# The samples' tile moved from the first prompt tile to the third, in a two-layer decoder step

## Chip, cores and metric

The kernel runs on all 8 cores of one Trainium2 chip. Each core does one prompt sequence of 2048 tokens and four of the 32 samples. The metric is device microseconds (us) of the slowest core. Executions come in two states: in the slow one, the cores of one die or of both have a lower granted TensorE clock, and the time is some per cent to over ten per cent longer.

## The reference, cut to what matters

One inference step of two layers is run for a prompt group and a sample group that share all weights.

```python
D_MODEL, SEQ, FFN_DIM = 1024, 2048, 2688
DEC_BATCH, DEC_SEQ, PAST_LEN = 32, 8, 8192
for layer in range(2):
    x = x + 0.5 * swiglu_ffn(rmsnorm(x), ...)        # FFN 0 / FFN 2
    h = rmsnorm(x)
    y = gla_mixer(h, ...) if layer == 0 \            # linear attention, carries a state
        else dilated_window_attention(q, shared_k, shared_v) @ w_o
    x = x + y
    x = x + 0.5 * swiglu_ffn(rmsnorm(x), ...)        # FFN 1 / FFN 3
    # after layer 0: the shared k, v are made from x
```

The samples start from a stored state (4 MB a core) and a stored window of keys and values. The kernel loads 13.6 MB of that window per core.

## The kernel before

The prompt is cut into four tiles of 512 tokens, t0 to t3. The core's samples form one more tile, ts, of 32 tokens. Two prompt tiles run side by side: t0 and t2 take their weights from ring 0, t1 and t3 from ring 1. Each ring holds 12,288 columns in SBUF, which is six units of 2048. All weights are loaded again for each prompt tile, as f32 in HBM and bf16 in SBUF. The samples have no weights of their own: they read the units of one prompt tile, each of which then has two users.

```python
for t in range(4):
    def add_unit(kind, i, src, n, users=0, t=t):
        u = Unit(src, n, users or (1 if t else 2), (t, kind, i))   # t0's units: t0 and ts
        ...
        order[t % 2].append(u)
    ...                                  # FFN 0; then v, qk of the linear attention
            if t == 0 and kind == "qk":  # the samples' state goes into the same ring
                for s in range(4):
                    add_unit("S0", s, src, 2048, 1)
    ...                                  # r, o; FFN 1; kv; FFN 2; wq
        if t == 0:                       # the samples' cache, before the output projection
            for s in range(4):
                add_unit("ck", s, ck[s], 3328, 1)
                add_unit("cv", s, cv[s], 3328, 1)
    ...                                  # wo; FFN 3

def weights(slot):                       # one such thread for each ring
    for k, u in enumerate(order[slot]):
        ...
        yield need(lambda over=over: all(o.left == 0 for _, _, o in over))  # all users done
        ...
        yield O(PL, lambda e: e.dma_start(out=dst, in_=u.src), ...)         # queue of POOL
        u.ready = True

def use(T, kind, i):
    u = units[(T.u, kind, i)]
    yield need(lambda: u.ready)
    ...
    return u
```

The program is written by threads (generators), one for each tile and many small ones. A greedy scheduler with a clock of its own picks, at each step, the operation that is ready first, and among nearly equal ones (`TIE = 0.15` us) the one of lowest rank. The samples' tile has the lowest rank of the tiles (-20), so it goes first. What comes out is a fixed order on each engine. On the chip every engine goes through its list in that order, and waits on semaphores.

```python
class Sched:
    DMA_BW = 315e3       # bytes per us
    DMA_LAT = 3.2        # us from the end of a transfer to its use
class Threads:
    TIE = 0.15
    FAVOUR = 0.02        # weight of rank against readiness on ACT and DVE
```

The samples' linear attention (`gla_s`) keeps its scratch in the key array `KT`, in the part of tiles t1 to t3, so that those tiles must not write their keys before it is done:

```python
KA, KB = KT[:, 0, 512:2048], KT[:, 1, 512:2048]
...
vv = KA[0:32, 0:1024]
...
# in kv(), before a prompt tile writes its keys
if T.t:
    yield need(lambda: "gla_s" in done)
```

The softmax here doesn't subtract the row's maximum and nothing guards it: scores larger than these inputs give would overflow.

Of the kernel before, what the change touches and what calls it, by code (L numbers as in the profile page):

```python
# [8 lines left out]
BF16 = mybir.dt.bfloat16  # L9
# [4 lines left out]
PE, ACT, DVE, PL, SP = ENGS  # L14
# [205 lines left out]
def O(eng, fn, reads=(), writes=(), cost=0.5, dma=None, nbytes=0):  # L220

    if fn.__closure__:
        fn = types.FunctionType(fn.__code__, fn.__globals__, fn.__name__, fn.__defaults__,
                                tuple(types.CellType(c.cell_contents) for c in fn.__closure__))
    return ("op", eng, fn, list(reads), list(writes), cost, dma, nbytes)


def need(cond):
    return ("need", cond)


def c_act(n):
    return 0.19 + n * 0.00084
# [76 lines left out]
def build():  # L310
# [20 lines left out]
    S = Sched(nc)  # L331
    TH = Threads(S)
    A = nc.alloc_sbuf_tensor
# [9 lines left out]
    KT = A("KT", [128, 2, 2048], BF16)  # L343
# [10 lines left out]
    PS = [PST[:, b, :] for b in range(8)]  # L354
# [81 lines left out]
    units = {}  # L436
    order = [[], []]

    for t in range(4):
        def add_unit(kind, i, src, n, users=0, t=t):  # L440
            u = Unit(src, n, users or (1 if t else 2), (t, kind, i))
            u.kind = kind
            units[(t, kind, i)] = u
            order[t % 2].append(u)

        def ffn_units(f):
            for j in range(NF):
                add_unit("fi%d" % f, j, wfi[f * NF + j], 2048)
            for m in range(8):
                add_unit("fo%d" % f, m, wfo[f * 8 + m], 2688)  # L450
                if (t, f) == (3, 3) and m % 2 == 0:

                    order[0].append(order[1].pop())
        ffn_units(0)
        for gi, kind in enumerate(("v", "qk", "r", "o")):
            for i in range(4):
                add_unit(kind, i, wgl[gi * 4 + i], 2048)
            if t == 0 and kind == "qk":
                for s in range(4):
                    src = st_in[s * 4:(s + 1) * 4].rearrange("h p d -> p h d")  # L460
                    add_unit("S0", s, src, 2048, 1)
                    add_unit("S0b", s, None, 1024, 1)
        ffn_units(1)
        for i in range(2):
            add_unit("kv", i, wkv[i], 2048)
        ffn_units(2)
        for i in range(3):
            add_unit("wq", i, wqd[i], 2048)
        if t == 0:
            for s in range(4):  # L470
                add_unit("ck", s, ck[s], 3328, 1)
                add_unit("cv", s, cv[s], 3328, 1)
        for i in range(4):
            add_unit("wo", i, wod[i], 1536)
        ffn_units(3)
# [52 lines left out]
    xsb = A("xsb", [128, 8, 32], F32)  # L528
    hsb = A("hsb", [128, 8, 32], BF16)
    spb = A("spb", [128, 10, 32], F32)  # L530
    rsb = A("rsb", [128, 1216], BF16)
    KTs = A("KTs", [128, 2, 32], BF16)
    Vsn = A("Vsn", [32, 256], BF16)
    stabs = A("stabs", [128, 64], F32)
    pool = Pool("pb", [pb[:, k, :] for k in range(NPB)])
# [4 lines left out]
    for t in range(4):  # L540
        T = Tile()
        i = t % 2
# [16 lines left out]
        tiles.append(T)  # L559
    TS = Tile()  # L560
    TS.nm, TS.i, TS.t, TS.n, TS.rank = "ts", "s", -1, 32, (lambda: -20)
    TS.u, TS.slot = 0, None
    TS.b = "bs"
    TS.x, TS.h, TS.pool = xsb, hsb, spool
    TS.R = rsb
# [8 lines left out]
    done = set()  # L574
# [7 lines left out]
    def rk(T, what):  # L582
        return ("R", T.b, what)
# [38 lines left out]
    def copy(eng, out, in_, n, reads, writes):  # L622
        if eng == ACT:
            return O(ACT, lambda e: e.copy(out=out, in_=in_), reads, writes, c_act(n))  # L624
        return O(eng, lambda e: e.tensor_copy(out=out, in_=in_), reads, writes, c_dve(n))
# [12 lines left out]


    def load_x(T, prev):  # L640
        nq = 4 if T.n == 512 else 1
        for q in range(nq):
            ms = range(q * 8 // nq, (q + 1) * 8 // nq)
            if prev is not None:
                yield need(lambda: all(("y", prev.nm, m) in done for m in ms))
            if T.t == 1:
                after = units[(0, "fi0", 3 + 2 * q)]
                yield need(lambda: after.ready)
            w = len(ms) * T.n
            src = xp[T.t] if T.n == 512 else xs  # L650
            yield O(ACT if T.t == 0 and q % 2 else SP, (lambda e, q=q, w=w, src=src, ms=ms: e.dma_start(
                out=T.x[:, ms[0]:ms[-1] + 1, :].rearrange("p m n -> p (m n)"), in_=src[:, q * w:(q + 1) * w])),
                [after.key] if T.t == 1 else [], writes=[xk(T, m) for m in ms], cost=0.1, dma="x%s_%d" % (T.b, q), nbytes=w * 512)
        if T.t == 0:

            T.sum = None
            for m in range(8):
                if m % 2:
                    yield stt(T.h[:, m, :], T.x[:, m, :], 1.0 / 1024, T.x[:, m, :], ALU.mult, ALU.mult, T.n, [xk(T, m)], [hk(T, m)])
                else:  # L660
                    yield act(T.h[:, m, :], T.x[:, m, :], AF.Square, T.n, [xk(T, m)], [hk(T, m)], scale=1.0 / 32)
                done.add(("sq", T.nm, 0, m))
            return
        for m in range(8):
            yield from square(T, m)
# [358 lines left out]
    def gla_s(T):  # L1024
        n = 32
        h8 = hks(T)
        R = T.R
        region(T, ACTK, ["g"])

        KA, KB = KT[:, 0, 512:2048], KT[:, 1, 512:2048]  # L1030
        qT = KB[:, 0:128].rearrange("p (h n) -> p h n", h=4)
        kT = KB[:, 128:256].rearrange("p (h n) -> p h n", h=4)
        kd = KB[:, 256:384].rearrange("p (h n) -> p h n", h=4)
        vv = KA[0:32, 0:1024]
        ktok = KA[0:32, 1024:1536].rearrange("p (h w) -> p h w", h=4)
        kms = KB[0:32, 384:896].rearrange("p (h w) -> p h w", h=4)
        am = KB[0:32, 896:1024].rearrange("p (h w) -> p h w", h=4)
        oT = R[:, 0:512].bitcast(F32).rearrange("p (m n) -> p m n", m=8)
        uT = R[:, 512:768].rearrange("p (m n) -> p m n", m=8)
        gk = rk(T, "g")  # L1040
# [4 lines left out]
        EQ, EK = A4, C4  # L1045
        (b,) = yield from get_banks(1)
        yield from mmh(T, (PS[b][0:16, 0:n],), lambda kt, z: WLR[:, kt, 0:16], ["WLR"], (b,), n)
        glr = KB[0:16, 896:928]
        yield copy(ACT, glr, PS[b][0:16, 0:n], n, [("ps", b)], [gk])
        put(b)  # L1050
        (b,) = yield from get_banks(1)
# [16 lines left out]
        for hd in range(4):  # L1068
            u = yield from use(T, "v", hd)
            v = u.ap.rearrange("p (kt c) -> p kt c", kt=8)  # L1070
            (b,) = yield from get_banks(1)
            yield mm(PS[b][0:32, 0:256], [(T.h[:, kt, :], v[:, kt, :]) for kt in range(8)], h8 + [u.key], b, 256)
            u.left -= 1
            yield copy(ACT, vv[:, hd * 256:(hd + 1) * 256], PS[b][0:32, 0:256], 256, [("ps", b)], [rk(T, ("gv", hd))])
            put(b)
        for hd in range(4):
            u = yield from use(T, "qk", hd)
# [29 lines left out]
        yield O(PE, fa, [gk], [("ps", b)], c_mm(4, 32))  # L1107
        yield tt(am, pa, CB[0:32, B_MS:B_MS + 32].unsqueeze(1).to_broadcast([32, 4, 32]), ALU.mult, 128, [("ps", b), "CB"], [gk])
        put(b)
        gv = [rk(T, ("gv", hd)) for hd in range(4)]  # L1110
        (b,) = yield from get_banks(1)

        def fi(e):
# [7 lines left out]
        for s in range(4):  # L1121
# [19 lines left out]
            for hp in range(2):  # L1141
# [10 lines left out]
                for a in range(2):  # L1152
                    hd = 2 * hp + a
# [3 lines left out]
                    cost=0.1, dma="sts%d" % s, nbytes=524288)  # L1157
            us.left -= 1
            ub.left -= 1

        sq = spb[:, 8:10, :].rearrange("p a n -> p (a n)").bitcast(BF16)
        RS = C4
# [7 lines left out]
        for hd in range(4):  # L1170
            u = yield from use(T, "r", hd)
# [13 lines left out]
        for q in range(4):  # L1185
            u = yield from use(T, "o", q)
# [4 lines left out]
                TH.spawn(resid(T, 2 * q + z, b, PS[b][:, 0:n], n), -4, T.rank)  # L1191
            u.left -= 1
        gs = ["g", "go", "kms"] + [("gv", h) for h in range(4)]
        for t in range(1, 4):
            for a in range(2):
                S.readers.setdefault(("KT", t, a), []).extend(
                    [S.lastw[rk(T, k)] for k in gs] + [r for k in gs for r in S.readers.get(rk(T, k), ())])
        region(T, gs, ACTK)
        done.add("gla_s")

# [35 lines left out]
    def kv(T, tab):  # L1236
        n = T.n
# [3 lines left out]
        def kpost(kc, b):  # L1241
            def write(t1, rs, k1, k2):
                yield tt(t1, t1, rs, ALU.mult, n, [k1, k2], [k1])
                if n == 512:
                    if T.t:
                        yield need(lambda: "gla_s" in done)
                    yield copy(ACT, KT[:, kc, T.t * 512:(T.t + 1) * 512], t1, n, [k1], [("KT", T.t, kc)])
                    dst = kp_o[kc][:, T.t * 512:(T.t + 1) * 512]
                else:
                    yield copy(ACT, KTs[:, kc, :], t1, n, [k1], [("KTs", kc)])  # L1250
                    dst = ks_o[kc]
                yield O(SP, (lambda e: e.dma_start(out=dst, in_=t1)), [k1], [], cost=0.1, dma="ko%s%d" % (T.b, kc), nbytes=n * 512)
                done.add(("K", T.nm, kc))
            yield from norm_rope(T, b, 62, tab, 3, write)
            left[0] -= 1
            if left[0] == 0 and tab[3] is not None:
                T.pool.put("tab", *tab[3])

        u = yield from use(T, "kv", 0)
# [6 lines left out]
        u = yield from use(T, "kv", 1)  # L1266
# [443 lines left out]
```

## Time and profile before

| | before |
|---|---|
| first three timed runs, us | 2356.7, 2508.9, 2710.3 |
| the profiled execution (fast), us | 2357.4 |
| span of the slowest core, us | 2355.6 (all: 2338.7 to 2355.6) |
| PE busy | 98% |
| granted clock, mean by core | 0.991 to 0.995 |

The page of the kernel before. First the busy time of each engine, then rows of busy tenths in 40 equal slices of the span (9 is 90% or more; PEclk is the granted clock, DMA the mean share of the 16 DMA engines), then the chain of work that ended last, by engine:

```profile
span 2355.6 us, 42703 instructions; the slowest of 8 cores (2338.7 to 2355.6 us)
PE 2298.3 (98%) x14643; PEld 1124.9 (48%) x14643; DVE 1218.2 (52%) x2181; ACT 1169.9 (50%) x2309; POOL 317.0 (13%) x599
...
PE   6999999999999999999999899999999999999998
...
PEclk9999999999999999999999999999999999999999
DMA  8997897888987999977999988888999989598793
...
PE 93%; DMA 5%; issue 1%; ACT 0%; DVE 0%; SPq 0%; DVEq 0%; POOLq 0%; ACTq 0%; POOL 0%
```

PE is the limit. A change can win only what PE waits. The view of waits lists the engine and line that waited, what released it, the total in us, the number of times and the longest. Here is PE in the kernel before:

```profile
PE pst L615 <- ACT hsb L620: 13.7, 1, 13.7
PE pst L615 <- DMA ring<-wfi: 8.2, 5, 3.7
PE pst L615 <- DVE h L631: 8.1, 5, 2.9
PE pst L615 <- DMA ring<-wfo: 8.0, 3, 7.4
...
PE pst L1523 <- DMA ring<-ck: 1.5, 1, 1.5
```

The first line is the start of the kernel. `wfi` and `wfo` are the FFN weights, `ck` the samples' cache. The timeline shows waits for weights (start us, length us, engine, line, operation, form, count, and the idle time before with its releaser). `hsb` and `rsb` belong to the samples, `h` and `r` to prompt tiles.

```profile
586.08 2.29 PE L615 MATMUL pst<-h,ring 128*128 128x512 bf16 x8
592.07 0.59 PE L615 MATMUL pst<-hsb,ring 128*128 128x32 bf16 x16 [3.70 <-DMA ring<-wfi]
592.49 2.72 PE L615 MATMUL pst<-h,ring 128*128 128x512 bf16 x6
...
849.43 3.62 PE L615 MATMUL pst<-h,ring 128*128 128x512 bf16 x16
854.58 0.97 PE L1523 MATMUL pst<-rsb,ring 64*128 64x8 bf16 x52 [1.53 <-DMA ring<-ck]
```

Sixteen matmuls of the samples take about 0.4 us from the first start to the next group, 25 ns each. Before them PE stood 3.70 us. The wait costs more than itself: during it the granted clock fell to 0.5, from 590.8 to 597.6 us, and the next eleven steps of the prompt matmuls took 427 ns in place of 216. The first line below is the stretch from 590 to 649 us; its mean clock is 0.94. The second is from tile t2's attention, which has room in DMA (columns: stretch, then busy us and count of PE, PEld, DVE, ACT, POOL, then granted clock, DMA share, GB/s):

```profile
590.00:649.00 59.00, 56.93 (x380) 27.33 (x381) 26.37 (x53) 34.23 (x74) 7.92 (x15) 0.94 0.95 157
2006.00:2065.00 59.00, 59.00 (x422) 30.29 (x421) 38.33 (x67) 34.95 (x68) 5.27 (x10) 0.97 0.60 102
```

### The profile page before, as it was taken

To read this page: it belongs to the slowest core of one execution; us is meant where nothing else is said; L and a number is where in the kernel's file an instruction comes from. 1 tells how busy PE (TensorE), PEld (TensorE's weight loads), DVE (VectorE), ACT (ScalarE), POOL (GpSimd) and SP (SyncE) were. 2 spreads that over 40 slices of the span, in tenths; PEclk is the share of its full clock that TensorE was granted. 3 is DMA by queue.
4 is the path that set the end of the run, shared out by engine and by line. 5 is a ranking of instruction groups with operands and counts; after the bars stand their busy time and mean duration, and the time that the engine had idled before them with its cause. 6 is when DMAs were issued, how large, how long until landed. Compare 5 with 4: busy or idle time off the path is not lost.

```text
span 2355.6 us, 42703 instructions; the slowest of 8 cores (2338.7 to 2355.6 us)
## 1 busy us (share of the span) xinstructions
PE 2298.3 (98%) x14643; PEld 1124.9 (48%) x14643; DVE 1218.2 (52%) x2181; ACT 1169.9 (50%) x2309; POOL 317.0 (13%) x599
## 2 busy tenths in 40 slices
PE   6999999999999999999999899999999999999998
PEld 3445455554445444445444355455444444544544
DVE  3535664566444566457442355644663355644732
ACT  4635655554543465555553156456555335644551
POOL 1111111111111111110111111111111111011010
PEclk9999999999999999999999999999999999999999
DMA  8997897888987999977999988888999989598793
GB/s 161 175 171 132 153 165 130 137 136 146 156 151 130 181 155 158 172 130 150 185 156 173 174 138 140 143 146 140 159 160 167 165 157 170 94 159 145 141 177 88
DMA packets 101475, 357.23 MB, mean 152 GB/s; under 512 B 12400, under 2 KB 17552, under 8 KB 101136
## 3 DMA queue, kind: packets, MB, share of 16 engines
q0 software_dynamic: 84144, 326.25, 83.1%
q1 hardware_dynamic: 16832, 27.21, 3.7%
q8 instruction: 122, 2.00, 0.3%
q10 hardware_dynamic: 288, 1.05, 0.2%
q14 instruction: 89, 0.73, 0.1%
HBM read 663.17 MB, written 15.40 MB: 288 GB/s over the span
## 4 chain that ended last, share of the span: by engine, by line
PE 93%; DMA 5%; issue 1%; ACT 0%; DVE 0%; SPq 0%; DVEq 0%; POOLq 0%; ACTq 0%; POOL 0%
PE pst L615 89%; DMA ring<-wfi 2%; DMA ring<-wfo 2%; PE pst L1436 1%; PE pst L1375 1%; DMA x<-xp 0%; DMA ring<-ck 0%; PE pst L1397 0%; PE pst L987 0%; PE pst L1004 0%; PE pst L1005 0%; ACT pb L620 0%; PE pst L1401 0%; PE pst L1459 0%; PE pst L974 0%
## 5 line engine op out<-in xcount | busy, mean ns | idle before, releaser
L615 PE MATMUL pst<-h,ring 128*128 128x512 bf16 x6144 | 1387.6, 381 | 9.4 <-DVE h L631 6.9
L615 PEld LDWEIGHTS pst<-h,ring 128*128 128x128 bf16 x6144 | 589.8, 98 | 707.4 <-issue 37.2
L615 PE MATMUL pst<-r,ring 128*128 128x512 bf16 x3136 | 707.2, 380 | 7.4 <-DMA ring<-wfo 7.4
L620 ACT ACTIVATE pb<-pb 128x512 f32<-128x512 f32 x856 | 535.4, 630 | 71.6 <-DVE pb L840 12.1
L620 ACT ACTIVATE pb<-pst 128x512 f32<-128x512 f32 (+1 forms) x472 | 278.9, 595 | 449.0 <-PE pst L615 441.8
L628 DVE TENSOR_TENSOR pb<-pb,pst 128x512 f32<-128x512 f32 x368 | 251.8, 685 | 463.8 <-ACT pb L620 456.4
L615 PEld LDWEIGHTS pst<-r,ring 128*128 128x128 bf16 x3136 | 302.1, 98 | 364.6 <-issue 12.8
L511 POOL DMA_DIRECT2D ring<-wfi x336 | 177.6, 529 | 1101.4 <-PE pst L615 973.7
L620 ACT ACTIVATE h<-x 128x512 bf16<-128x512 f32 x188 | 116.6, 627 | 353.7 <-DVE x L631 280.2
L628 DVE TENSOR_TENSOR r<-pb,pst 128x512 bf16<-128x512 f32 x336 | 230.5, 686 | 46.3 <-DVE pb L628 38.8
L631 DVE SCALAR_TENSOR_TENSOR x<-pst,x 128x512 f32<-128x512 f32 x128 | 88.2, 689 | 216.4 <-PE pst L615 215.7
L631 DVE SCALAR_TENSOR_TENSOR h<-x,CF,pb 128x512 bf16<-128x512 f32 x224 | 150.8, 745 | 12.4 <-ACT pb L620 9.4
L511 POOL DMA_DIRECT2D ring<-wfo x128 | 67.6, 528 | 540.7 <-PE pst L615 439.4
L628 DVE TENSOR_TENSOR pb<-pb,h 128x512 f32<-128x512 f32 x115 | 79.0, 689 | 44.8 <-ACT h L620 42.6
L615 PE MATMUL pst<-ring,h 128*128 128x256 bf16 x640 | 74.4, 273 | 0.0
L620 ACT ACTIVATE spb<-pst 128x32 f32<-128x32 f32 (+2 forms) x111 | 21.7, 198 | 100.5 <-PE pst L615 99.2
L615 PEld LDWEIGHTS pst<-hsb,ring 128*128 128x128 bf16 x1536 | 52.4, 96 | 32.2 <-issue 13.8
L615 PEld LDWEIGHTS pst<-ring,h 128*128 128x128 bf16 x640 | 62.3, 98 | 11.2
L511 POOL DMA_DIRECT2D ring<-wgl x64 | 33.8, 530 | 220.3 <-PE pst L615 201.6
L624 ACT COPY r<-pst 128x512 f32<-128x512 f32 (+3 forms) x104 | 51.2, 492 | 23.6 <-PE pst L1401 11.3
L615 PE MATMUL pst<-hsb,ring 128*128 128x32 bf16 x1536 | 54.0, 177 | 8.3 <-DMA ring<-wfi 8.2
L620 ACT ACTIVATE h<-pst 128x512 bf16<-128x512 f32 (+4 forms) x96 | 46.4, 510 | 18.3 <-PE pst L1375 10.3
(153 smaller groups left out, 1082.5 us busy)
## 6 DMA issues: line engine op xcount, KB each, us to landing
ring<-wfi POOLq DMA_DIRECT2D x336, 512.0 KB, 7.8
ring<-wfo POOLq DMA_DIRECT2D x128, 672.0 KB, 8.2
ring<-wgl POOLq DMA_DIRECT2D x64, 512.0 KB, 7.2
y_p<-x SPq DMA_DIRECT2D x32, 256.0 KB, 8.1
x<-xp SPq DMA_DIRECT2D x14, 512.0 KB, 10.4
ring<-wqd POOLq DMA_DIRECT2D x12, 512.0 KB, 10.5
ring<-wod POOLq DMA_DIRECT2D x16, 384.0 KB, 7.6
ring<-wkv POOLq DMA_DIRECT2D x8, 512.0 KB, 7.3
```

The costliest lines, as they stand in the source:

```text
L511: yield O(PL, (lambda e, u=u, dst=dst: e.dma_start(out=dst, in_=u.src)), first.get(u.uid, []), writes=[u.key], cost=1.0, dma="w%d_%d" % (s ...
L615: ins = e.matmul(out, lhsT=l, rhs=r, start=(start and i == 0), stop=(stop and i == last), skip_group_check=skip)
L620: return O(ACT, lambda e: e.activation(out=out, in_=in_, func=func, scale=scale, bias=bias), reads, writes, c_act(n))
L624: return O(ACT, lambda e: e.copy(out=out, in_=in_), reads, writes, c_act(n))
L628: return O(DVE, lambda e: e.tensor_tensor(out=out, in0=a, in1=b, op=op), reads, writes, c_dve(n, rate))
L631: return O(DVE, lambda e: e.scalar_tensor_tensor(out=out, in0=a, scalar=s, in1=b, op0=op0, op1=op1), reads, writes, c_dve(n))
L1375: ins = e.matmul(PS[bs[hp]][:, bi * 256 + jj * 128:bi * 256 + jj * 128 + 128], lhsT=KT[hp * 64:hp * 64 + 64, jj, sl_(k0, 128, kst)], rhs=T ...
L1436: ins = e.matmul(PS[bs[hp]][0:nk, rr * 64 + jj * 32:rr * 64 + jj * 32 + 32], lhsT=KT[hp * 64:hp * 64 + 64, jj, sl_(r, nk, 16)], rhs=T.QT[h ...
```

## The change

The intent is to take the samples' loads (their state and cache) and their latencies out of the crowded first tile and put them where the prompt's attention is long and DMA has room. Tile t2's weights get the second user. The samples start when t0 is done. Their scratch shrinks to the last tile's part of `KT`, which is free longest; the values go to one of the 11 shared scratch buffers, and only t3 must wait for `gla_s`.

```diff
+    TSU = 2
     for t in range(4):
         def add_unit(kind, i, src, n, users=0, t=t):
-            u = Unit(src, n, users or (1 if t else 2), (t, kind, i))
+            u = Unit(src, n, users or (2 if t == TSU else 1), (t, kind, i))
 ...
-            if t == 0 and kind == "qk":
+            if t == TSU and kind == "qk":
 ...
-        if t == 0:
+        if t == TSU:
             for s in range(4):
                 add_unit("ck", s, ck[s], 3328, 1)
 ...
-    TS.u, TS.slot = 0, None
+    TS.u, TS.slot = TSU, None
 ...
     def load_x(T, prev):
+        if T.n == 32:
+            yield need(lambda: ("y", "t0", 0) in done)
 ...
-        KA, KB = KT[:, 0, 512:2048], KT[:, 1, 512:2048]
+        KA, KB = KT[:, 0, 1536:2048], KT[:, 1, 1536:2048]
+        (vi,) = yield from pool.get(("s", "vv"), 1, 1)
 ...
-        vv = KA[0:32, 0:1024]
+        vv = pool.aps[vi][0:32, :].bitcast(BF16)
 ...
-                    if T.t:
+                    if T.t == 3:
                         yield need(lambda: "gla_s" in done)
```

Cut: the places of the smaller scratch arrays, `rsb` longer by 64 columns, and the order of reads and writes for the smaller region.

More of the change, by code (lines that the diff above doesn't have):

```diff
@@ L530, in build @@
     spb = A("spb", [128, 10, 32], F32)
-    rsb = A("rsb", [128, 1216], BF16)
+    rsb = A("rsb", [128, 1280], BF16)
     KTs = A("KTs", [128, 2, 32], BF16)
@@ L1028, in gla_s @@
         region(T, ACTK, ["g"])
-        KA, KB = KT[:, 0, 512:2048], KT[:, 1, 512:2048]
-        qT = KB[:, 0:128].rearrange("p (h n) -> p h n", h=4)
-        kT = KB[:, 128:256].rearrange("p (h n) -> p h n", h=4)
-        kd = KB[:, 256:384].rearrange("p (h n) -> p h n", h=4)
-        vv = KA[0:32, 0:1024]
-        ktok = KA[0:32, 1024:1536].rearrange("p (h w) -> p h w", h=4)
-        kms = KB[0:32, 384:896].rearrange("p (h w) -> p h w", h=4)
-        am = KB[0:32, 896:1024].rearrange("p (h w) -> p h w", h=4)
+        KA, KB = KT[:, 0, 1536:2048], KT[:, 1, 1536:2048]
+        (vi,) = yield from pool.get(("s", "vv"), 1, 1)
+        qT = KA[:, 0:128].rearrange("p (h n) -> p h n", h=4)
+        kT = KA[:, 128:256].rearrange("p (h n) -> p h n", h=4)
+        kd = KA[:, 256:384].rearrange("p (h n) -> p h n", h=4)
+        am = KA[0:32, 384:512].rearrange("p (h w) -> p h w", h=4)
+        ktok = KB[0:32, :].rearrange("p (h w) -> p h w", h=4)
+        vv = pool.aps[vi][0:32, :].bitcast(BF16)
+        vk = pool.key(vi)
+        kms = R[0:32, 768:1280].rearrange("p (h w) -> p h w", h=4)
         oT = R[:, 0:512].bitcast(F32).rearrange("p (m n) -> p m n", m=8)
@@ L1047, in gla_s @@
         yield from mmh(T, (PS[b][0:16, 0:n],), lambda kt, z: WLR[:, kt, 0:16], ["WLR"], (b,), n)
-        glr = KB[0:16, 896:928]
+        glr = KA[0:16, 384:416]
         yield copy(ACT, glr, PS[b][0:16, 0:n], n, [("ps", b)], [gk])
@@ L1073, in gla_s @@
             u.left -= 1
-            yield copy(ACT, vv[:, hd * 256:(hd + 1) * 256], PS[b][0:32, 0:256], 256, [("ps", b)], [rk(T, ("gv", hd))])
+            yield copy(ACT, vv[:, hd * 256:(hd + 1) * 256], PS[b][0:32, 0:256], 256, [("ps", b)], [vk, rk(T, ("gv", hd))])
             put(b)
@@ L1109, in gla_s @@
         put(b)
-        gv = [rk(T, ("gv", hd)) for hd in range(4)]
+        gv = [vk] + [rk(T, ("gv", hd)) for hd in range(4)]
         (b,) = yield from get_banks(1)
@@ L1159, in gla_s @@
             ub.left -= 1
+        pool.put(("s", "vv"), vi)
         sq = spb[:, 8:10, :].rearrange("p a n -> p (a n)").bitcast(BF16)
@@ L1193, in gla_s @@
         gs = ["g", "go", "kms"] + [("gv", h) for h in range(4)]
-        for t in range(1, 4):
-            for a in range(2):
-                S.readers.setdefault(("KT", t, a), []).extend(
-                    [S.lastw[rk(T, k)] for k in gs] + [r for k in gs for r in S.readers.get(rk(T, k), ())])
+        for a in range(2):
+            S.readers.setdefault(("KT", 3, a), []).extend(
+                [S.lastw[rk(T, k)] for k in gs] + [r for k in gs for r in S.readers.get(rk(T, k), ())])
         region(T, gs, ACTK)
```

## The prediction

> All times are for the fast state (2356.7 us timed, 2357.4 profiled; the other two timed runs, 2508.9 and 2710.3, I take as slow).
>
> **What bounds the kernel now.** PE. The page gives PE 98% busy in a 2355.6 us span; the chain of waits is 93% PE. Busy time proves little (the Trainium skill, "Perfetto Trace Analysis", opening note, calls it a bad metric), so I read the starts of successive matmuls in the timeline: 216 ns for 128x512, 109 for 128x256, 25 for the samples' 128x32. That agrees with the floor of about 25 ns in the Trainium skill, "TensorE: Matmul & The Clock Gate", section "Wait — 56ns, not 53.3ns?". With each form at its median step, PE needs about 2244 us. So only some 111 us are not needed: 13.7 before the first matmul, 6.3 after the last, about 91 between. The change can win or lose only there.
>
> Where the 91 lie: 17 in the first 120 us (half-rate matmuls of 427 ns up to about 28 us, waits for weights and norm); 7 at 540-600 (waits for weights); 14.4 at 840-960, where the samples' attention waits for its cache (chain: 10.8 us of loading it; DMA 0.89 to 1.0); 14.3 at 1320-1380, where tile 1 ends and tile 3 starts (7.6 us wait for FFN output weights, DMA 0.99); 17 in the attention of tiles 2 and 3 (1980-2040 and 2160-2220; waits for ACT and DVE).
>
> **What moves.** Nothing is removed: the same matmuls, the same bytes. The samples' 2320 FFN-type matmuls at 25 ns are 58 us, their whole PE work some 75 us by the same steps; it leaves the first 1100 us and comes back between about 1000 and 2200. So do 4 state loads of 1 MB and 8 cache loads of 1.7 MB, 17.8 MB of HBM reads; at the mean 288 GB/s an estimated 62 us of loading. One of 11 shared scratch buffers is held during the samples' linear attention. The wait on its completion is left to tile 3 and should cost nothing: tile 3's keys come over 400 us of PE work later in program order.
>
> **On the critical path.**
> - Gain, 6 to 12 us: the cache loads leave tile 0's short attention, where DMA is full, for that of tile 2, where DMA is at 0.60 (2006-2065 us). Most of the 14 us at 840-960 goes.
> - Gain, 2 to 5 us: the samples' short matmuls fill part of the wait at the tile 1 to tile 3 change, and of the waits in tile 2's attention.
> - Loss, 4 to 8 us: in the first 180 us DMA is at 0.90 to 1.03, and the samples' 13 us of first-FFN work filled PE there. Without it PE waits longer for weights.
> - Loss, 0 to 4 us: the samples' small ACT and DVE operations (about 200 ns each) meet tile 2's attention, which already waits for ACT and DVE; one scratch buffer fewer.
>
> Sum: about -7 us. Predicted **2350 us**, 8 in 10 between **2330 and 2372**. Faster by over 2%: 0.03; within 2%: 0.94; slower by over 2%: 0.03.
>
> **What would show it.** Right: the same PE work; waits on the cache near tile 0's attention gone, no equal one at tile 2's; a few us more waiting for weights before 180 us; tile 0 ends some 70 us earlier; DMA near tile 2's attention up from 0.60.
>
> **What would make it wrong.** The cache loads hold tile 2's half of the weight ring so long that its output projection waits (PE idle over 15 us near 1950-2050); state loads colliding with the tile 1 to tile 3 change, already at DMA 0.99; the first 180 us losing over 15 us, DMA-bound.

## The result, and the profile after

Ratios in this document are the mean time of one kernel's fast runs over that of the other's in the same rounds, so they are not quite the ratio of the medians quoted.

| | before | after |
|---|---|---|
| first rounds, fast runs, us | 2356.7, 2358.8 | 2354.2 to 2358.5 (4 runs, median 2356.1) |
| ratio, 95% interval | | 0.9993 (0.9969 to 1.0018) |
| five more rounds, median of fast runs, us | 2357.0 | 2355.7 |
| ratio, 95% interval | | 0.9994 (0.9980 to 1.0008) |
| profiled span, slowest core, us | 2355.6 | 2354.4 |
| PE busy on that core, us | 2298.3 | 2300.7 |

The time is the same: 1.4 us less in the longer measurement, with an interval from 4.7 less to 1.9 more (the ratios times 2357). The medians of all runs of the first rounds, 2433.9 before and 2356.1 after, differ because two of the four runs before were slow; that says nothing about the change.

The page after:

```profile
span 2354.4 us, 42684 instructions; the slowest of 8 cores (2335.8 to 2354.4 us)
PE 2300.7 (98%) x14643; PEld 1124.7 (48%) x14643; DVE 1220.7 (52%) x2181; ACT 1167.7 (50%) x2309; POOL 317.0 (13%) x599
...
PE   6999999999999999999998999999999999999998
...
PEclk9999999999999999999999999999999999999999
DMA  9999799799989899799898898888898899997793
...
PE 91%; DMA 7%; issue 1%; ACT 1%; DVE 0%; POOL 0%; DVEq 0%; SPq 0%; ACTq 0%; POOLq 0%
```

The same number of matmuls, the same busy time. DMA's share of the chain is larger, 7% against 5%. The view of waits for PE after (lines shifted by 2):

```profile
PE pst L617 <- ACT h L622: 13.0, 1, 13.0
PE pst L617 <- DMA ring<-wfi: 9.5, 6, 4.8
PE pst L617 <- DMA ring<-wfo: 9.0, 7, 4.0
PE pst L617 <- DVE h L633: 5.7, 3, 2.7
PE pst L617 <- DVE r L630: 4.2, 2, 2.3
```

The wait for the cache (`ck`) is gone. The waits for FFN weights are not less: 18.5 us in 13 pieces (9.5 + 9.0), against 16.2 in 8. The timeline after shows the same picture as before, a thousand us later:

```profile
1700.70 2.41 PE L617 MATMUL pst<-h,ring 128*128 128x512 bf16 x8
1704.86 0.55 PE L617 MATMUL pst<-hsb,ring 128*128 128x32 bf16 x16 [1.75 <-DMA ring<-wfi]
...
1244.77 4.48 PE L617 MATMUL pst<-r,ring 128*128 128x512 bf16 x20
1253.27 0.72 PE L617 MATMUL pst<-rsb,ring 128*128 128x32 bf16 x21 [4.02 <-DMA ring<-wfo]
```

And the queue of POOL just before the first of these (here POOL's own lines; the idle time in brackets is what POOL waited for before it could issue the load):

```profile
1693.49 0.53 POOL L513 DMA_DIRECT2D ring<-wfi  x1 [5.05 <-PE pst L617]
1697.41 1.05 POOL L513 DMA_DIRECT2D ring<-wfi  x2 [3.40 <-PE pst L617]
```

The load that PE waits for is one of the two issued at 1697.41, and POOL could not issue it earlier because PE still held the place in the ring. It was in use 7.4 us later. So the ring is full. The samples read at its front, the prompt tile lets go at its back, and PE, in program order, stands at the samples' matmuls until the load has landed.

The stretch of t2's attention, after (columns as before; this window is the one in which the samples' attention runs):

```profile
1960.00:2040.00 80.00, 78.10 (x967) 42.91 (x963) 48.81 (x100) 50.51 (x123) 12.13 (x23) 0.91 1.02 163
```

DMA there went from 0.60 to 1.02, as the intent has it, with PE still busy 78.1 of 80 us. The windows are not of equal length: over the wider stretch from 1960 to 2065 us the kernel before had 0.72.

### Where PE waits, phase by phase

Busy time can't show this, so I worked out a table from the starts of successive matmuls. Each form has a usual step (216 ns for 128x512, 25 ns for the samples' 128x32, the median over all traces). What a step takes beyond that is called a wait here. It includes steps at half clock. The phases end at the last matmul of a stage of t0, t1 or t2, so whatever runs beside is counted too. Values are us, the mean of the six cores whose traces hold all 14,643 matmuls (two lack some 260). Single figures move by up to 2 us between two profiles of the same kernel, and the sum by 4.

| phase | before | after | after, second profile |
|---|---|---|---|
| S: start to the end of t0's FFN 0 | 27.6 | 30.8 | 29.3 |
| A1: beside t0, linear attention to FFN 2 | 13.7 | 3.2 | 3.2 |
| A2: beside t0, attention, output projection, FFN 3 | 17.4 | 8.6 | 7.8 |
| X: t1 ends, t3 starts, to the end of t2's FFN 0 | 10.2 | 7.2 | 6.2 |
| B1: beside t2, linear attention to FFN 2 | 4.9 | 18.1 | 16.2 |
| B2: beside t2, attention, output projection, FFN 3 | 10.9 | 14.8 | 15.7 |
| sum | 84.6 | 82.7 | 78.4 |

This is where the gain went: 20 us of waits left t0, and 17 us appeared beside t2. Counting the 128x512 steps of 400 to 450 ns in the same traces, about 12 of the 85 us before, and 13 to 15 after, are the excess of half-clock steps and not standing still; in B1 it is 1.3 us before, 3.3 and 2.7 after.

The waits can also be split by the tile whose matmul ends them. A recount for B1 (its usual steps differ a little, which adds 2 us to every B1):

| B1, wait before a matmul of | samples | t2 | t3 |
|---|---|---|---|
| before | 0 | 4.0 | 3.0 |
| after (second profile) | 8.5 (7.4) | 3.8 (3.6) | 7.8 (7.3) |
| follow_after (below) | 1.9 | 6.1 | 2.8 |
| no_samples (below) | 0 | 2.0 | 8.2 |

So about 8 us of the rise stand before the samples' matmuls; single waits for weights of over 0.25 us make up about half of that. Another 4 to 5 us stand before t3's, which read the other ring; the longest, 2.3 us in t3's first FFN, is a wait for DVE (`DVE r` in the view above). The 8.2 us of no_samples lie elsewhere, at t3's start.

### The profile page after: what moved, and what is told of

Its sections match the earlier page's. It is cut to its first block, busy times and chain, and to the rows that moved or that the text cites. A ratio compares the mean times of both kernels' runs of the same rounds, so it can differ in the third digit from the quotient of the medians.

```text
span 2354.4 us, 42684 instructions; the slowest of 8 cores (2335.8 to 2354.4 us)
## 1 busy us (share of the span) xinstructions
PE 2300.7 (98%) x14643; PEld 1124.7 (48%) x14643; DVE 1220.7 (52%) x2181; ACT 1167.7 (50%) x2309; POOL 317.0 (13%) x599
## 4 chain that ended last, share of the span: by engine, by line
PE 91%; DMA 7%; issue 1%; ACT 1%; DVE 0%; POOL 0%; DVEq 0%; SPq 0%; ACTq 0%; POOLq 0%
PE pst L617 87%; DMA ring<-wfo 3%; DMA ring<-wfi 3%; PE pst L1442 1%; PE pst L1381 0%; PE pst L1403 0%; DMA ring<-wkv 0%; DMA x<-xp 0%; ACT pb L622 0%; PE pst L991 0%; PE pst L1008 0%; PE pst L1009 0%; PE pst L1407 0%; PE pst L1465 0%; PE pst L826 0%
## 5 line engine op out<-in xcount | busy, mean ns | idle before, releaser
L617 PEld LDWEIGHTS pst<-hsb,ring 128*128 128x128 bf16 x1536 | 52.1, 96 | 28.8 <-issue 10.1
L622 ACT ACTIVATE h<-pst 128x512 bf16<-128x512 f32 (+4 forms) x96 | 46.2, 509 | 17.5 <-PE pst L1381 9.5
```

The source lines that it names most:

```text
L617: ins = e.matmul(out, lhsT=l, rhs=r, start=(start and i == 0), stop=(stop and i == last), skip_group_check=skip)
L622: return O(ACT, lambda e: e.activation(out=out, in_=in_, func=func, scale=scale, bias=bias), reads, writes, c_act(n))
```

## The experiments

Theory A: the samples bring their waits with them, because they are the first reader of each unit of a full ring. Theory B: the bytes of the state and cache fill DMA, whoever reads. Theory C: the scratch buffer taken from the pool. Theory D: the cache stands in the ring before the output projection's weights. Theory E: any change of the fixed order trades waits among the phases. The phases S to B2 of the table above are used throughout.

### The changed kernel again

> The changed kernel again, in five rounds, to size the difference. My record said 7 us less than before (ratio 0.997); the first rounds gave 0.9993. By the phase table of the two traces (mean of six cores) the span changed by -2 us. Theory A and B both expect 0.9975 to 1.000.

Measured: 0.9994 (0.9980 to 1.0008), as said above. This is within both theories. The 7 us lie outside the interval.

### The samples follow the prompt tile

```diff
 def use(T, kind, i):
-        yield need(lambda: u.ready)
+        yield need(lambda: u.ready and (T.n == 512 or u.left == 1))
```

Beside t2 (the changed kernel):

> The changed kernel, but the samples' tile may use a shared weight unit only after the third prompt tile has used it. Theory A (the samples' tile has the highest rank and is the first reader of every unit of its ring, so PE, which goes in program order, stands at its matmuls until the load has landed): PE waits in the phases from tile 2's linear attention to its third FFN fall from 18 us to under 9, and the time falls by 6 to 12 us against the changed kernel. Theory B (DMA is full there because of the samples' state and cache loads, whoever reads the weights first): those waits stay at 15 us or more and only change their names to tile 2's matmuls; time within 3 us.

Beside t0 (the kernel before):

> The kernel before, with the same rule beside tile 0. Theory A: the waits in the phases from tile 0's linear attention to its output projection (20 us) fall by 6 to 12 us and the time is 0.995 to 0.9975 of before. Theory B: within 3 us of before.

| | time ratio to before | A1 | A2 | B1 | B2 |
|---|---|---|---|---|---|
| after | 0.9994 | 3.2 | 8.6 | 18.1 | 14.8 |
| follow_after | 1.0014 (1.0001 to 1.0028) | 3.2 | 7.9 | 8.7 | 28.0 |
| before | 1 | 13.7 | 17.4 | 4.9 | 10.9 |
| follow_before | 0.9999 (0.9985 to 1.0012) | 7.6 | 25.9 | 4.8 | 11.6 |

The waits that theory A explains fell as it says, from 18.1 to 8.7 beside t2 and from 13.7 to 7.6 beside t0. The time did not. 13 us came back in the attention phase beside t2, and 8.5 beside t0. A sample tile that follows reaches its attention late: it starts at 1959 us in place of 1942 (mean of six cores), and t2's output projection starts 5 us later although t2's own attention ends 8 us earlier. That its cache units hold the ring meanwhile is the likely reason, argued and not tested alone. In the view of waits of follow_after the wait for the cache is back:

```profile
PE pst L1529 <- DMA ring<-ck: 2.6, 1, 2.6
```

So theory A holds for the waits before the samples' own matmuls in B1 (8.5 to 1.9 us). Those before t3's fell too (7.8 to 2.8), for a reason not shown. My expectation that removing the cause would remove time was wrong.

### No samples at all

```diff
-            u = Unit(src, n, users or (1 if t else 2), (t, kind, i))
+            u = Unit(src, n, users or 1, (t, kind, i))
 ...  # no state units, no cache units, no wait on gla_s
-    for T, prev in ((tiles[0], None), (TS, None), (tiles[1], None), ...):
+    for T, prev in ((tiles[0], None), (tiles[1], None), ...):
```

> The samples' tile, its state and its cache are left out (their outputs stay unwritten, wrong on purpose). Both theories: 75 us of PE work goes; the start waits as in the changed kernel (31 us until tile 0's first input half, against 27 before), since the samples are missing there too. Waits from tile 0's linear attention to its output projection: under 9 us (20 before); from tile 2's linear attention to its third FFN: under 8 us (18 after). Time about 2265 us, 2255 to 2275.

Measured: 0.9638 of before, 2272 us, the samples' outputs wrong on purpose. S is 29.1, A1 3.1, A2 7.8, X 12.1, B1 8.1, B2 16.5. S, A1 and A2 are those of the changed kernel: what moved away from t0 moved away wholly, and the start is longer by what the samples used to fill. Without samples X is 12.1 and with them beside t2 it is 6 to 7, so they do fill the change of tiles. B1 was expected under 8 and is 8.1, and B1 and B2 together are 24.6, against 15.8 in the kernel before, though none of that work differs. By this run, about half of what appeared beside t2 does not need the samples at all (a later run takes most of that half back).

### The scratch alone

```diff
-    TSU = 2
+    TSU = 0
     def load_x(T, prev):
-        if T.n == 32:
-            yield need(lambda: ("y", "t0", 0) in done)
```

> The second half of the change alone: the scratch lies as in the changed kernel (last tile's part of the keys, one shared buffer for the values, the wait on its completion left to tile 3), but the samples stay beside tile 0. If the scratch and its waits matter little: 0.999 to 1.001 of before, waits from tile 0's linear attention to its output projection 18 to 22 us as before. If the one shared buffer costs something: 3 us or more of extra waits in tile 0's linear attention.

Measured: 1.0005 (0.9988 to 1.0022). A1 is 13.5 (13.7 before), B1 4.8 (4.9). The second half of the change has no effect of its own, good or bad.

### The values in a place of their own

```diff
-        (vi,) = yield from pool.get(("s", "vv"), 1, 1)
-        vv = pool.aps[vi][0:32, :].bitcast(BF16)
-        vk = pool.key(vi)
+        vv = Vg1[0:32, 2].rearrange("p r w -> p (r w)")
+        vk = ("Vg1", 2)
```

> The changed kernel, but the samples' values lie in the third slot of the gathered values (free until tile 2 writes it) and no shared buffer is held. Theory C (the buffer taken from the pool is what adds waits beside tile 2's linear attention): that phase falls from 10 us to under 6 us and the time by 3 to 6 us. Theory A (first reader of the weights): within 2 us of the changed kernel, that phase stays at 8 us or more.

Measured: 0.9990 (0.9978 to 1.0002), B1 17.6; in the phase of t2's linear attention alone the wait was 9.7 us as in the changed kernel. Theory C falls.

### The loads alone

```diff
 # the kernel without samples, with the state and cache units back beside t2, read by nobody
 # (and without the empty places S0b that held a bf16 copy of the state)
-            if False and kind == "qk":
+            if t == 2 and kind == "qk":
 ...
+            if kind in ("S0", "S0b", "ck", "cv"):
+                u.left = 0
```

> No samples' tile, but its state and cache are loaded into the ring beside tile 2, unused (wrong on purpose). Theory B (bytes alone make the waits): waits from tile 2's linear attention to its third FFN rise from 8 us without samples to 14 us or more. Theory A: they stay under 10 us. Theory D (the cache loads stand in the ring before tile 2's output projection weights): waits in the phases of tile 2's output projection and fourth FFN rise above the 17 us seen without samples, to 20 or more. Time 2268 to 2280 us.

Measured: 0.9638 of before, the same as without samples and without these loads. B1 is 8.0 (8.1 without the loads). Theory B falls: 17.8 MB more of loading from HBM made no PE wait in B1. B2 is 18.4 against 16.5, under the 20 of theory D. As long as nobody has to read the cache before its place is free again, it holds up little.

### The samples follow in the first two FFNs only

```diff
-        yield need(lambda: u.ready)
+        yield need(lambda: u.ready and (T.n == 512 or kind[-1] not in "01" or u.left == 1))
```

> As follow_after, but the rule holds in the first two FFNs only, so that the samples can run ahead again in the third FFN and ask for their cache early. follow_after took 18 us of waits down to 9 between tile 2's linear attention and its third FFN, and gave 13 us back at the output projection and fourth FFN. If that give-back comes from the samples reaching their attention late: the first part stays (that sum 8 to 12 us), the second goes (15 us, as in the changed kernel), and the time is 5 to 9 us under the changed kernel. If the waits only change place: within 3 us of the changed kernel.

Measured: 1.0031 (0.9998 to 1.0064). The waits in B2 stayed low (16.9), as expected, but B1 did not keep its gain: 17.5. The part of FFN 2 in it rose from 5.9 to 9.5 us. This expectation failed. The waits only changed place: 9.3 us of B1 again stand before the samples' matmuls, which run ahead in that FFN.

### A margin for the samples, and a later landing for all

```diff
 # margin_*: the samples use a unit 6 us after the scheduler's landing
+        yield need(lambda: u.ready and (T.n == 512 or u.src is None or S.lastw[u.key][3] + 6.0 <= S.free[PE]))
 # late_*: every load is believed to land later
-    DMA_LAT = 3.2
+    DMA_LAT = 8.0
```

> The changed kernel, with the samples' use of a weight placed in program order at least 6 us (by the scheduler's own clock) after the load is believed to have landed. Theory A (PE stands at the samples' matmuls because they are placed right behind the landing, and a load of the full ring is issued only when tile 2 lets go of a unit): the waits from tile 2's linear attention to its third FFN fall from 18 to under 11 us and, unlike follow_after, the samples stay ahead of tile 2, so the output projection and fourth FFN stay at 15 to 17 us; time 4 to 8 us less than the changed kernel. Theory E (the waits depend on how the two prompt tiles fall against each other, and any shift of the order trades one for another): sums of waits within 4 us of the changed kernel's 80 to 84, time within 4 us.

> The kernel before with the same margin. Theory A: waits from tile 0's linear attention to its third FFN fall from 14 to under 8 us, time 3 to 7 us less than before. Theory E: time within 4 us of before.

> The changed kernel; the scheduler takes 8.0 us in place of 3.2 us from the end of a load's transfer to its use, for every load (the profile has 7 to 10 us from issue to landing), so every first use is placed later. Theory A: weight waits go for all tiles, time 5 to 12 us less than the changed kernel. Theory E: within 4 us.

> The kernel before with 8.0 us in place of 3.2 us. Theory A: 5 to 12 us less than before. Theory E: within 4 us. With both kernels so corrected, the place of the samples should matter as the start and tile 0's attention say: beside tile 2 4 to 8 us less than beside tile 0.

| | ratio to before | A1 | A2 | B1 | B2 | sum |
|---|---|---|---|---|---|---|
| margin_after | 1.0040 (0.9962 to 1.0119) | 3.2 | 9.1 | 10.8 | 32.5 | 91.9 |
| margin_before | 0.9994 (0.9950 to 1.0037) | 8.9 | 28.9 | 4.7 | 11.5 | 89.1 |
| late_after | 0.9968 (0.9906 to 1.0030) | 1.7 | 8.9 | 10.1 | 19.8 | 80.3 |
| late_before | 0.9970 (0.9926 to 1.0014) | 5.0 | 25.6 | 4.8 | 9.9 | 85.8 |

This chip gave many slow runs and the intervals are wide; one run of the kernel before that counts as fast took 2382 us, which lowers all four ratios. No pair differs clearly: the two late kernels have 0.9968 and 0.9970. The phases are clear: in all four kernels the waits in the FFN stages beside the samples fall (18 to 10 or 11 in B1, 14 to 5 or 9 in A1), and in all four the following attention phase gets longer. The view of waits of margin_after on core 1, from 1925 to 2120 us, shows what late sample attention goes with. The kernel had put t2's output projection, which ended at about 2085 us, into t3's attention, and PE waits for weights, DVE and ACT by turns:

```profile
PE pst L617 <- DMA ring<-wfo: 5.5, 1, 5.5
PE pst L617 <- DVE h L630: 2.6, 1, 2.6
PE pst L1381 <- ACT pb L622: 2.1, 1, 2.1
PE pst L617 <- DVE x L630: 1.5, 1, 1.5
```

In the changed kernel, the same view of the same core and stretch has one line, 0.4 us:

```profile
PE pst L1403 <- ACT h L622: 0.4, 1, 0.4
```

### The noise of the order itself

```diff
-    TIE = 0.15          # tie_*
+    TIE = 0.2
-    FAVOUR = 0.02       # favour_*
+    FAVOUR = 0.03
```

> A control for the noise of the order itself: the kernel before with the scheduler's window for ties at 0.20 us in place of 0.15; nothing else. Theory E (any new order trades waits among the phases): the time differs from before by 2 to 8 us either way, and single phases by 3 us or more. If the order is not that sensitive: within 2 us and 2 us in every phase.

> The changed kernel with the same window of 0.20 us. If the move of the samples has a value of its own of 7 us, as I recorded, this is 4 to 10 us under tie_before. If it has none beyond the order's noise: between 5 us under and 5 us over it.

> Second control: the kernel before with the weight of rank against readiness on ACT and DVE at 0.03 in place of 0.02. Theory E: differs from before by 2 to 8 us either way, phases by 3 us or more.

> The changed kernel with 0.03. A value of its own of the move: 4 to 10 us under favour_before. None: within 5 us of it. In both pairs the waits beside tile 0 (linear attention to fourth FFN) should be lower with the samples beside tile 2, as in the first pair (31 against 13), and the waits beside tile 2 higher.

| | ratio to before | S | A1 | A2 | X | B1 | B2 |
|---|---|---|---|---|---|---|---|
| tie_before | 1.0017 (1.0004 to 1.0031) | 26.7 | 12.1 | 18.0 | 9.7 | 4.9 | 15.0 |
| tie_after | 0.9995 (0.9979 to 1.0012) | 30.3 | 1.7 | 8.3 | 8.2 | 18.4 | 14.4 |
| favour_before | 0.9997 (0.9985 to 1.0010) | 27.0 | 10.4 | 18.9 | 9.8 | 5.6 | 10.1 |
| favour_after | 0.9986 (0.9972 to 1.0000) | 29.3 | 3.1 | 8.4 | 7.4 | 15.7 | 19.6 |

A tie-break constant alone moves the time by up to 0.17% (4 us, tie_before) and single stages by more: t0's attention and output projection had 6.4 us of waits before and 13.6 with FAVOUR at 0.03, most of it won back in the next stage. Over the three pairs the move to t2 is worth 1.4, 5.2 and 2.6 us (differences of the ratios times 2357). Each is in the predicted direction, and the last two lie on either side of the 4 us line that I had drawn. The phases repeat in all three pairs: A1 falls by 7 to 10.5 us, A2 by 9 to 10.5, B1 rises by 10 to 13.5. B2 is not steady: it changes by +4, -0.6 and +9.5.

### Without samples, with the other window for ties

The edit is the kernel without samples with `TIE = 0.2`.

> The kernel without samples, with the window for ties at 0.20. Without samples the phases from tile 2's linear attention to its fourth FFN had 25 us of waits, the kernel before 16 (and 20 with this window), though none of that work differs. If the 9 us belong to the missing samples: 24 us or more again. If to the order: 15 to 21 us. Waits beside tile 0 (linear attention to fourth FFN) 9 to 12 us either way. Time 2268 to 2277 us.

Measured: 0.9626 of before, 2271 us. B1 is 8.0 and B2 10.9, together 18.9, against 24.6 with the old window. So B2 is the order's noise: the same work, a different tie-break, 5.6 us. Nearly as much came back in X, which rose from 12.1 to 16.8. B1 is 8.0 in all three kernels without samples and 4.7 to 5.6 in those with samples beside t0. Nearly all of the 3 us lie at the change of tiles, in the 10 us just behind the line between X and B1, where 7.1 us are lost without samples and 4.5 in the kernel before. Without samples it is t3's first norm and first FFN input that wait there, mostly for DVE; before, it was t2's norm. Why is left open.

### The later landing once more

> The changed kernel with 8.0 us of load latency in the scheduler again: it had the lowest times of all (2353 us against 2360 us for before on that chip), but its interval was wide. If that is a gain of its own: 0.996 to 0.998 of before with an interval under 1. If it was the chip: 0.998 to 1.000.

Measured: 0.9973 (0.9958 to 0.9987), median of fast runs 2354.3 against 2359.8 us on that chip. The changed kernel with 8.0 us for the landing came out 6 to 8 us faster than the kernel before, twice, the second time with an interval under 1. That it beats the changed kernel is not shown: the two were never timed in the same rounds. On this chip the kernel before itself was 2 us slower in these rounds than in those of the tie-break (mean of fast runs 2359.6 and 2357.6), and favour_after came to 2354.1 against 2353.4 here. Nor is it shown that the gain needs the move, since late_before had the same ratio as late_after and was not repeated. The sum of PE waits, the mean of six cores, does not show it (83.7 and 80.3, against 82.7 and 78.4 for the changed kernel), so what makes it faster than the kernel before on the slowest core is not explained here.

## Why the prediction was right or wrong

It said 2350 us, 7 less than before. The time came out at 2356, within its range, but the 7 us were not there: the five-round measurement has 1.4 less, at most 4.7. Point by point, with the first pair of phases (before against the mean of the two profiles after):

- *PE bounds, and only its waits can be won.* Right. PE's work was the same, 2298.3 and 2300.7 us busy, and the 75 us of samples' work went and came back. Without samples the time falls by 85 us. t0 ended about 115 us earlier (mean of six cores), not 70; the waits that left with the samples' work make up 20 of these.
- *Gain of 6 to 12 us at t0's attention.* Right in size: A2 fell by 9.2 us, in the other two pairs by 9.7 and 10.5. The cache found room beside t2, where DMA rose from 0.60 to 1.02. The reason given is only in part shown: of the 17.4 us before, 2.7 stood before the samples' matmuls and about 1.5 were waits for the cache; most of what went stood before t0's and t1's. No run moved the cache alone.
- *Gain of 2 to 5 us at the change of tiles and in t2's attention.* Right for the first: X fell by 3.5. Without samples it is 12 to 17. The second is not seen: B2 rose.
- *Loss of 4 to 8 us at the start.* Right in kind, too large: S rose by 2.5 us. The kernels without samples have about the same start (29.1) as the changed one (30.8 and 29.3).
- *Loss of 0 to 4 us beside t2.* This is the step that failed. It was written as "the samples' small ACT and DVE operations [...] meet tile 2's attention, which already waits for ACT and DVE; one scratch buffer fewer". Beside t2, 16.6 us appeared (12.3 in B1, 4.4 in B2). Neither the buffer (vv_own) nor the scratch (scratch_only) nor the bytes (loads_only) is the reason. The attention part, B2, is about the size I gave, and it is within the noise of the order. The larger part, B1, lies in the stages before the attention, from the linear attention to the third FFN, where I had looked for nothing. About 8 us of it stand before the samples' own matmuls, which read a full ring first, and they go when the samples no longer read first (1.9 us left in follow_after; B1 as a whole is 9 to 11 there and in margin_after and late_after). The rest stands before t3's matmuls, in part as waits for DVE, and its cause stays open.
- The same oversight stands on the other side: I had listed 7 us of waits at 540-600 and did not ask who was waiting. It was the samples, and those waits moved too. A1 fell by 10.5 us, a gain that was not in the sum. The two errors nearly cancel (12.3 against 10.5).

With the measured sizes, -9.2 - 3.5 + 2.5 + 4.4 + 12.3 - 10.5 = -4.0 us in the mean of six cores' waits. The time, that of the slowest core, has 1 to 5 us less over the three pairs. That the time still lies within the range is in this sense luck: two terms of 10 to 12 us, one left out and one put at 0 to 4, nearly cancelled. The gain I forecast was thus not lost at one place. It was small, one of its terms was traded for another, and its size is that of the noise which the new orders tried here bring.

What the experiments settle: the scratch and the pool cost nothing measurable, and the bytes nothing in B1; the samples' weight waits come from their being first at a full ring; and putting the samples later removes those waits and pays for it in the attention phase. What stays open: the waits before t3's matmuls in B1, which of the samples' loads and operations made the waits in A2, and why the later landing is faster than the kernel before on the slowest core.

## What to carry to other kernels

When a small tile shares weights with a large one, ask which of the two reads at the front of the ring: its waits go where it goes, and the large tile's matmuls behind it in program order wait with it. Before forecasting a gain of a few us from moving work in a statically scheduled kernel, change one tie-break constant and see how far the time moves; a gain of that size needs several orders, not one, to be shown. And list every wait with its waiter, since a wait that belongs to the moved work is not removed by the move.

## What the Trainium skill lacked or had wrong

- "TensorE: Matmul & The Clock Gate", section "Seeing it yourself": it says to budget 13/16 of the clock, 1.95 GHz, for sustained dense matmul on all cores. Here the cores were 97 to 98% busy with matmuls for 2350 us at a granted clock of 0.990 to 0.995 (means by core in the first profiles of both kernels, in the fast state). In slow runs one die or both fell: in two runs of one kernel (favour_after) one die had means of 0.94 to 0.95 and of 0.86 to 0.87, with the other at 0.99; in a run of the kernel before of 2716 us both had 0.84 to 0.87. The page does not say that both states happen to one program. It speaks of the default power profile; which one this chip has is not on record.
- The same page, section "Wait — 56ns, not 53.3ns?": the floor of about 25 ns from start to start, "however small N is", agrees for the samples' 128x32, which had 25 ns. It is not the floor of every small matmul here: in the samples' attention 52 matmuls with 64 columns of weights (128*64 in the profile) began within 0.85 us, 16 ns each.
- "DMA: Bandwidth & Descriptors", section "Anatomy of one DMA — SWDGE (gpsimd) path": its fit of 2.0 us plus bytes over 436 GB/s gives, as an estimate, 4.4 us for a unit of 1 MB read. In this kernel, with DMA queues busy 87 to 90% of the span, the FFN input units, which are of that size, took a median of 7.8 us from issue to landing before the change and 8.9 after. No page gives this time for engines so busy, and a scheduler needs it. The model here has 3.2 us after a transfer that it puts at 3.3 us (1 MB at 315 GB/s), 6.5 in all.
- No page says how much a static order alone is worth: 0.17% of the time (tie_before), and up to 7 us of waits in one stage (favour_before), from one constant of the scheduler each.
